# A streaming encoder layer on one core: transposed rows for a triangular solve, 32x32 tiled products, signs on ScalarE, and a head fed by two queues

## The chip, the core and the metric

The kernel runs on one core of one Trainium2 chip. The metric is device time in microseconds (us) of one execution; the time before is the median of three executions. All data are float32. TensorE is called PE below, VectorE DVE, ScalarE ACT, GpSimd POOL and SyncE SP.

## The reference

One layer of a hybrid encoder over 256 time steps of width 2048. Two recurrent mixers (a gated linear recurrence, "LRU", and RWKV-7 with 32 heads of 64) read columns of one input projection; a cross-attention over 256 memory tokens and a SwiGLU follow, each behind a layer norm. Cut to what matters here:

```
h = layer_norm(x, ln_in_g, ln_in_b)
zin = h @ w_in
u, gate_lru, z_rw, g_a, g_b = split(zin)
y_a = gelu(gate_lru) * rg_lru(conv(u))
y_b = rwkv7_time_mix(z_rw)
h = LN1(ALPHA*h + (sig(g_a)*y_a + sig(g_b)*y_b) @ w_out)
h = LN2(ALPHA*h + cross_attention(h, mem))     # k = mem @ wk
h = LN3(ALPHA*h + (silu(h @ wg) * (h @ wu)) @ wd)

# inside rwkv7_time_mix
kf = kf * (1.0 + (a - 1.0) * k_a)
def step(S, inp):
    r_t, w_t, k_t, v_t, kk_t, b_t = inp
    sa = einsum('bhvk,bhk->bhv', S, kk_t)
    S = S * w_t - sa * b_t + v_t * k_t          # outer products per head
    return S, einsum('bhvk,bhk->bhv', S, r_t)
```

The kernel computes the RWKV steps in four chunks of 64 time steps. Within a chunk the steps depend on each other through a unit lower triangular 64x64 matrix per head, and the kernel inverts it.

## The kernel before

**Weights.** Every weight matrix is streamed once, in "halves" of 128x1024 floats (512 KB). `split_half` loads a half on SP's queue (`raw`, L152, four buffers), ACT rounds it to a shorter format (`wh`, L155) and DVE subtracts that from the raw half (`wl`, L157, three buffers for the pair). PE then does eight products of 128x128 with `wh` and 512 columns (L168) and eight with `wl` and 256 columns (L171). Two halves make a 128-wide column block of a projection (`wtile`); ACT copies one part of the sum out of PSUM (`jl`, L183) and DVE adds the other (`js`, `ur`, L186). The output projection, the values, the attention output and the last projection use L202, L203 and L206 with the operands exchanged.

**Stages.** The head loads the memory (`mraw`, L314, four DMAs of 512 KB on SP's queue), splits it in the same manner (ACT L328, DVE L330 into the tiles `m`), computes NB0 = 3 of the 16 key blocks of the cross-attention from it, normalizes x (transposes L256), and computes NB1 = 5 keys in all; these "early keys" are written to DRAM and read back later. Then come four small projections, and four RWKV groups of four 128-wide blocks (eight heads) each, between which the LRU blocks and the gates are placed. After these stand the output projection, the first norm, the cross-attention with the keys that are left, the second norm, the SwiGLU and the last norm.

**The solve of a group.** When the last products of a group (`gt`, L507) are there, `recurrence` writes the 32x32 diagonal blocks of the triangular matrices to DRAM (`scr`, L535) and reads them back as `al`, one system per partition, 32x32 floats each, matrix row index s ahead of column index t (L541). DVE sets the diagonal (L545) and does 31 steps of a triangular inversion: a product `pd` of the part of the inverse that is known with column t of `al` (L552), and a sum over it, `xi` (L555). Element (s, t) of `al` lies 32 floats from (s+1, t), so L552 reads that operand with a stride of 128 bytes. The inverse goes through DRAM once more (`scx`, L558) into `ymat` (L563).

**After the solve.** `chunk_steps` runs when `PACE` (20, 28, 20, 20) more halves have passed. DVE transposes the upper diagonal blocks into `x1z` (L570). PE multiplies them with the off-diagonal blocks (L576), ACT copies the result out (`zz`, L580), PE multiplies with the lower diagonal blocks (L585), and DVE writes the negative of that into `ymat` (L589). `x1z`, `zz` and `ymat` are padded with zeros, so that each 32x32x32 product runs over all 128 rows of the array. Then come four chunks in turn: products L608, ACT copy `rhsz` (L611), products with `ymat` (L615), DVE's negative of that (`sv`, L617), the state (L624 and DVE), products L633 and ACT's copy `ott` (L635). The group norm (L642 is one of its steps) and a gate finish the group.

**Order.** A scheduler sorts each engine's instructions ahead of time by priorities (`tc.cur_priority`, `stream`, `ahead`) and by `defer(n, fn)`, which lets `fn` run after n more halves. On the chip every engine works through its list in that order and waits on semaphores; an instruction that waits holds up all behind it on its engine.

The L552 step reads, with `al` as `[partition, s, t]`:

```
nc.vector.tensor_tensor(pd[:, 0:nj, 0:t + 1], xi[:, 0:nj, 0:t + 1],
                        al[:, 0:t + 1, t].rearrange("p (o s) -> p o s", o=1)
                        .broadcast_to([P, nj, t + 1]), ALU.mult)
nc.vector.tensor_reduce(xi[:, 0:nj, t], pd[:, 0:nj, 0:t + 1], AX.X, ALU.add, negate=True)
```

Of the kernel before, what the change touches and what calls it, by code (L numbers as in the profile page):

```python
# [18 lines left out]
P = 128  # L19
T = 256  # L20
# [11 lines left out]
NB0, NB1 = 3, 5  # L32
XP, CP = 4, 5
# [13 lines left out]
def trunk(ctx, tc, x, memT, vec, rows, consts, lruw, loraw, w_in, w_out, wq, wk, wv, wo, wgu, wd, out,  # L47
# [113 lines left out]

    def wstat(src, xh, xl, acc):
        for hf in range(2):
            h, l = split_half(src, hf)
            for kk in range(8):
                k = hf * 8 + kk
                w = h[:, kk * P:(kk + 1) * P]
                nc.tensor.matmul(acc, w, both[id(xh[k])], start=(k == 0), stop=False)  # L168
            for kk in range(8):
                k = hf * 8 + kk  # L170
                mm = nc.tensor.matmul(acc[:, 0:T], l[:, kk * P:(kk + 1) * P], xh[k], start=False,  # L171
                                      stop=(k == 15))
            passed(mm.ins)
# [4 lines left out]
    def wtile(src, xh, xl, out=None):  # L178
        a = new_acc()
        wstat(src, xh, xl, a)  # L180
        with stream(32):
# [109 lines left out]
    with ExitStack() as mx:  # L291
# [15 lines left out]
        st = wk1.tile([P, 2, 4, 6], F32, name="st")  # L307
        with ahead():
            mraw = []
            for hf in range(2):  # L310
                tc.cur_priority = 65 + hf
                m = boot.tile([P, 8, T], F32, name=f"mraw{hf}")
                for q in range(2):
                    nc.sync.dma_start(m[:, 4 * q:4 * q + 4], memT[:, 8 * hf + 4 * q:8 * hf + 4 * q + 4, :])  # L314
                mraw.append(m)
        tc.cur_priority = 64 * XP + 1
        for tt in range(2):
            for hf in range(2):
                cs = slice(hf * 1024, (hf + 1) * 1024)
                nc.sync.dma_start(xt[:, tt, cs], x[tt * P:(tt + 1) * P, cs])  # L320
        tc.cur_priority = 64 * CP + 2
        nc.sync.dma_start(vt, vec)
        nc.sync.dma_start(ct, consts)
        tc.cur_priority = 1001000
        mTh, mTl = pair_tiles(boot, NK, "m")
        for k in range(NK):
            src = mraw[k // 8][:, k % 8, :]
            nc.scalar.copy(mTh[k], src)  # L328
            eng = nc.gpsimd if k % 4 == 3 else nc.vector
            eng.tensor_tensor(mTl[k], src, mTh[k].bitcast(F32), ALU.subtract)  # L330

# [5 lines left out]
        for k in range(NB0):  # L337
            early_key(k)
# [21 lines left out]
        x1z = grp.tile([P, 2, 16, 32], F32, name="x1z")  # L360
        nc.gpsimd.memset(x1z, 0.0)
        zz = grp.tile([P, 2, 16, 32], F32, name="zz")
        nc.gpsimd.memset(zz, 0.0)
# [78 lines left out]
        def tile_stage(g, j, i, u, fs, av, ev, dt, kr, bkt, sv, yb, gt):  # L442
# [3 lines left out]
            def key_direction():  # L446
# [22 lines left out]
                nc.vector.tensor_scalar(kf, av, col("k_a", i), oka[:, i:i + 1], ALU.mult, ALU.add)  # L469
# [57 lines left out]
        def recurrence(g, kkr, gt, bkt, sv, dm, yb, scr, scx, pace):  # L527
# [17 lines left out]
            nc.vector.memset(al.rearrange("p s t -> p (s t)")[:, 0:1024:33], -1.0)  # L545
# [21 lines left out]
        def chunk_steps(g, kkr, gt, bkt, sv, dm, yb, gi):  # L567
            for pr in range(2):
                q = 64 * (1 - pr)
                nc.vector.transpose(x1z[q:q + 32, pr], ymat[q:q + 32, :, 0:32])  # L570
            psz = rps()
            for pr in range(2):
                q = 64 * (1 - pr)
                for it in range(16):
                    lhsT = gi[:, it // 2, (it % 2) * 2 + pr, q + 32:q + 64]
                    nc.tensor.matmul(psz[q + 32:q + 64, it * 32:(it + 1) * 32], lhsT, x1z[:, pr, it, :],  # L576
                                     start=True, stop=True, skip_group_check=True)
            for pr in range(2):
                q = 64 * (1 - pr)
                nc.scalar.copy(zz[q + 32:q + 64, pr].rearrange("p i t -> p (i t)"), psz[q + 32:q + 64, :])  # L580
            psy = rps()
            for pr in range(2):
                q = 64 * (1 - pr)
                for it in range(16):
                    nc.tensor.matmul(psy[q:q + 32, it * 32:(it + 1) * 32], zz[:, pr, it, :], ymat[:, it, 32:64],  # L585
                                     start=True, stop=True, skip_group_check=True)
            for pr in range(2):
                q = 64 * (1 - pr)
                nc.vector.tensor_scalar(ymat[q:q + 32, :, 32:64],  # L589
                                        psy[q:q + 32, :].rearrange("p (i t) -> p i t", i=16), -1.0, None, ALU.mult)  # L590
# [5 lines left out]
            for c in range(4):  # L596
# [20 lines left out]
                nc.vector.tensor_scalar(sv[q0:q0 + 64, c, :], pss[q0:q0 + 64, :], -1.0, None, ALU.mult)  # L617
# [430 lines left out]
```

## Time and profile before

| what | value |
|---|---|
| time, median of 3 executions | 2145.86 us (2145.09 to 2146.47) |
| the profiled execution's own time | 2147.81 us |
| its span, first to last instruction | 2146.0 us |
| PE busy | 97% of the span |
| DVE busy | 69% |
| ACT busy | 51% |
| POOL busy | 5% |
| mean granted clock of TensorE | 0.991 of full speed |

The span is the time between the first and the last instruction in the profile; the execution's own time is 1.8 us longer. "Busy" is the time in which at least one instruction of an engine was running, and is an average over all stages. A wait is counted for the engine that stood still, and put down to the instruction that released it. In the timeline, a row stands for a run of equal instructions: start, duration from the first start to the last end, engine, line, operation, result and operands, count, and in square brackets the idle time ahead of the row with what ended it. The granted clock of TensorE has two levels, 1.2 and 2.4 GHz; a stretch's PEclk is the mean over it, with 1.00 for 2.4 GHz throughout.

### The profile page before, as it was taken

To read this page: it belongs to the slowest core of one execution; us is meant where nothing else is said; L and a number is where in the kernel's file an instruction comes from. 1 tells how busy PE (TensorE), PEld (TensorE's weight loads), DVE (VectorE), ACT (ScalarE), POOL (GpSimd) and SP (SyncE) were. 2 spreads that over 40 slices of the span, in tenths; PEclk is the share of its full clock that TensorE was granted. 3 is DMA by queue.
4 is the path that set the end of the run, shared out by engine and by line. 5 is a ranking of instruction groups with operands and counts; after the bars stand their busy time and mean duration, and the time that the engine had idled before them with its cause. 6 is when DMAs were issued, how large, how long until landed. Compare 5 with 4: busy or idle time off the path is not lost.

```text
span 2146.0 us, 31754 instructions
## 1 busy us (share of the span) xinstructions
PE 2078.3 (97%) x12176; PEld 1782.4 (83%) x12176; DVE 1472.4 (69%) x2341; ACT 1092.3 (51%) x1658; POOL 117.4 (5%) x162
## 2 busy tenths in 40 slices
PE   7999999999999998999999999999999999999996
PEld 6888788888887887878888888788888888888885
DVE  7888878978795887677864665685555555545545
ACT  6756645565563574564644544454444444443332
POOL 2200010011002000200000000000000000000001
PEclk9999999999999999999999999999999999999998
DMA  8545535544553465386565444565555555555553
GB/s 292 197 157 178 174 111 163 176 145 150 178 175 111 145 189 171 126 280 238 183 210 193 166 142 168 177 217 200 191 187 187 188 190 191 187 190 193 195 192 123
DMA packets 139192, 387.74 MB, mean 181 GB/s; under 512 B 38560, under 2 KB 47648, under 8 KB 138272
## 3 DMA queue, kind: packets, MB, share of 16 engines
q1 hardware_dynamic: 127664, 360.42, 49.4%
q0 software_dynamic: 4384, 14.16, 2.1%
q10 hardware_dynamic: 6992, 11.14, 1.7%
q8 instruction: 95, 1.56, 0.3%
q14 instruction: 57, 0.47, 0.1%
HBM read 375.05 MB, written 10.62 MB: 180 GB/s over the span
## 4 chain that ended last, share of the span: by engine, by line
PE 81%; DVE 10%; DMA 4%; issue 2%; ACT 2%; SPq 0%; POOL 0%; ACTq 0%; DVEq 0%; POOLq 0%
PE acc L168 33%; PE acc L171 17%; PE acc L206 7%; PE acc L202 7%; PE acc L203 7%; DVE wl L157 3%; DVE pd L552 1%; DMA gb<-in_rows_dram 1%; ACT wh L155 1%; DVE xi L555 1%; PE rec L608 1%; PE rec L633 1%; PE rec L615 1%; DMA mraw<-in_memT_dram 1%; PE mix L507 1%
## 5 line engine op out<-in xcount | busy, mean ns | idle before, releaser
L157 DVE TENSOR_TENSOR wl<-raw,wh 128x1024 fp32r<-128x1024 f32 x656 | 801.3, 1223 | 512.8 <-ACT wh L155 485.9
L155 ACT CAST wh<-raw 128x1024 fp32r<-128x1024 f32 x656 | 685.0, 1047 | 651.8 <-PE acc L203 255.7
L168 PE MATMUL acc<-xT,wh 128*128 128x512 f32 x3520 | 914.3, 399 | 10.0 <-DVE js L186 7.7
L168 PEld LDWEIGHTS acc<-xT,wh 128*128 128x128 f32 x3520 | 636.6, 190 | 128.8 <-DVE js L186 9.4
L171 PEld LDWEIGHTS acc<-xT,wl 128*128 128x128 f32 x3520 | 483.0, 191 | 36.4 <-DVE wl L157 0.8
L171 PE MATMUL acc<-xT,wl 128*128 128x256 f32 x3520 | 503.0, 284 | 0.0
L203 PE MATMUL acc<-wh,f 128*128 128x512 f32 x352 | 136.9, 389 | 0.0
L202 PE MATMUL acc<-wh,f 128*128 128x512 f32 x352 | 136.9, 389 | 0.0
L206 PE MATMUL acc<-wl,f 128*128 128x512 f32 x352 | 108.4, 389 | 0.0
L183 ACT COPY jl<-acc 128x256 f32<-128x256 f32 x236 | 86.5, 367 | 24.5 <-PE acc L171 23.8
L186 DVE TENSOR_TENSOR js<-acc,jl 128x256 f32<-128x256 f32 x215 | 89.9, 418 | 5.5 <-ACT jl L183 5.0
L203 PEld LDWEIGHTS acc<-wh,f 128*128 128x128 f32 x352 | 66.1, 188 | 13.8
L206 PEld LDWEIGHTS acc<-wl,f 128*128 128x128 f32 x352 | 66.1, 188 | 13.7
L202 PEld LDWEIGHTS acc<-wh,f 128*128 128x128 f32 x352 | 66.0, 188 | 13.6
L552 DVE TENSOR_TENSOR pd<-xi,al 128x2 f32<-128x2 f32 (+30 forms) x124 | 63.0, 508 | 2.3
L202 PE MATMUL acc<-wh,A 128*128 128x512 f32 x128 | 50.4, 394 | 2.9 <-ACT wh L155 2.9
L203 PE MATMUL acc<-wh,A 128*128 128x512 f32 x128 | 50.3, 393 | 0.0
L202 PE MATMUL acc<-wh,oT 128*128 128x512 f32 x128 | 50.0, 391 | 0.0
L203 PE MATMUL acc<-wh,oT 128*128 128x512 f32 x128 | 49.8, 389 | 0.0
L203 PE MATMUL acc<-wh,B 128*128 128x512 f32 x128 | 49.8, 389 | 0.0
L202 PE MATMUL acc<-wh,B 128*128 128x512 f32 x128 | 49.8, 389 | 0.0
L913 ACT ACTIVATE fsg<-js 128x256 f32<-128x256 f32 x44 | 18.4, 417 | 55.7 <-DVE js L186 55.5
(266 smaller groups left out, 2135.3 us busy)
## 6 DMA issues: line engine op xcount, KB each, us to landing
raw<-in_w_in_dram SPq DMA_DIRECT2D x232, 512.0 KB, 3.5
raw<-in_wgu_dram SPq DMA_DIRECT2D x176, 512.0 KB, 3.5
raw<-in_wd_dram SPq DMA_DIRECT2D x88, 512.0 KB, 3.5
raw<-in_wk_dram SPq DMA_DIRECT2D x32, 512.0 KB, 4.0
raw<-in_w_out_dram SPq DMA_DIRECT2D x32, 512.0 KB, 4.4
raw<-in_wv_dram SPq DMA_DIRECT2D x32, 512.0 KB, 4.0
raw<-in_wq_dram SPq DMA_DIRECT2D x32, 512.0 KB, 3.5
raw<-in_wo_dram SPq DMA_DIRECT2D x32, 512.0 KB, 3.5
```

The source lines that it names most:

```text
L155: nc.scalar.copy(h, raw)
L157: nc.vector.tensor_tensor(l, raw, h.bitcast(F32), ALU.subtract)
L168: nc.tensor.matmul(acc, w, both[id(xh[k])], start=(k == 0), stop=False)
L171: mm = nc.tensor.matmul(acc[:, 0:T], l[:, kk * P:(kk + 1) * P], xh[k], start=False, stop=(k == 15))
L183: nc.scalar.copy(t, a[:, T:2 * T])
L186: nc.vector.tensor_tensor(out, a[:, 0:T], t, ALU.add)
L202: nc.tensor.matmul(pt[tt], xh[k][:, ts], w, start=(first and kk == 0), stop=False)
L203: nc.tensor.matmul(pt[tt], xl[k][:, ts], w, start=False, stop=False)
L206: nc.tensor.matmul(pt[tt], xh[k][:, ts], l[:, kk * 512:(kk + 1) * 512], start=False, stop=(last and kk == 1))
L507: nc.tensor.matmul(pt[hh][:, c * P:(c + 1) * P], q["bk"][rows, c, :], kr[rows, c, :], start=True, stop=True)
L552: nc.vector.tensor_tensor(pd[:, 0:nj, 0:t + 1], xi[:, 0:nj, 0:t + 1], al[:, 0:t + 1, t].rearrange("p (o s) -> p o s", o=1) .broadcast_to([ ...
L555: nc.vector.tensor_reduce(xi[:, 0:nj, t], pd[:, 0:nj, 0:t + 1], AX.X, ALU.add, negate=True)
```

## The change

1. **The solve.** A new tile `at_` holds `al` with s and t exchanged. ACT copies it, all 128x1024 elements, writing with the stride. The diagonal is set in `at_`, and each step reads a row of `at_`, in which neighbours are 4 bytes apart.
2. **The off-diagonal products.** The 32x32 products run in 32x32 tiles of the array (`tile_position`), over 32 rows and without padding. The row pairs alternate product by product, between rows 64 and 0 of the array in the first burst and rows 96 and 32 in the second, and both pairs write one PSUM tile (`psz`, `psy`), as they did before. `x1z` and `zz` give way to one tile `xz`.
3. **Signs and a key step on ScalarE.** The negatives for `ymat` (8 instructions) and `sv` (16), and `kf` = `av` x k_a + oka (16), move from DVE to ACT activations.
4. **The head.** The memory's DMAs are issued on ACT's queue, beside the weights on SP's. Fourteen products of zeros stand at the start of PE's list. Keys 0 and 1 are computed half by half: the first halves of both, which need the first half of the memory alone, and then the second halves. Casts of the memory get priorities between those of the weights, the loads of x are spread between weights, and the small constants change places. NB0 and NB1 become 4 and 7.

```diff
-NB0, NB1 = 3, 5
+NB0, NB1 = 4, 7
...
+        zw = boot.tile([P, P], F32, name="zw")
+        nc.gpsimd.memset(zw, 0.0)
+        zp = rps()
         with ahead():
+            for _ in range(14):
+                nc.tensor.matmul(zp[:, 0:P], zw, zw, start=True, stop=True, skip_group_check=True)
...
-                tc.cur_priority = 65 + hf
+                tc.cur_priority = 65 + 2 * hf
...
-                    nc.sync.dma_start(m[:, 4 * q:4 * q + 4], memT[:, 8 * hf + 4 * q:8 * hf + 4 * q + 4, :])
+                    nc.scalar.dma_start(m[:, 4 * q:4 * q + 4], memT[:, 8 * hf + 4 * q:8 * hf + 4 * q + 4, :])
...
+        krs = [boot.tile([P, T], F32, name="kr", bufs=2) for _ in range(2)]
+        ac = [new_acc() for _ in range(2)]
+        for hf in range(2):
+            for k in range(2):
+                wstat_half(wk[k], mTh, mTl, ac[k], hf)
+        for k in range(2):
+            joined(ac[k], krs[k])
+            nc.sync.dma_start(k_d[k], krs[k])
+        for k in range(2, NB0):
             early_key(k)
...
-                nc.vector.tensor_scalar(kf, av, col("k_a", i), oka[:, i:i + 1], ALU.mult, ALU.add)
+                nc.scalar.activation(kf, av, AF.Identity, scale=col("k_a", i), bias=oka[:, i:i + 1])
...
-            nc.vector.memset(al.rearrange("p s t -> p (s t)")[:, 0:1024:33], -1.0)
+            at_ = grp.tile([P, 32, 32], F32, name="at")
+            nc.scalar.copy(at_.rearrange("p t s -> p s t"), al)
+            nc.vector.memset(at_.rearrange("p t s -> p (t s)")[:, 0:1024:33], -1.0)
...
-                                        al[:, 0:t + 1, t].rearrange("p (o s) -> p o s", o=1)
+                                        at_[:, t, 0:t + 1].rearrange("p (o s) -> p o s", o=1)
...
-                nc.vector.transpose(x1z[q:q + 32, pr], ymat[q:q + 32, :, 0:32])
+                nc.vector.transpose(xz[q:q + 32], ymat[q:q + 32, :, 0:32])
             psz = rps()
+            for it in range(16):
+                for pr in range(2):
+                    q = 64 * (1 - pr)
+                    nc.tensor.matmul(psz[q + 32:q + 64, it * 32:(it + 1) * 32],
+                                     gi[q:q + 32, it // 2, (it % 2) * 2 + pr, q + 32:q + 64], xz[q:q + 32, it, :],
+                                     start=True, stop=True, skip_group_check=True, tile_position=(q, q + 32))
...
-                for it in range(16):
-                    lhsT = gi[:, it // 2, (it % 2) * 2 + pr, q + 32:q + 64]
-                    nc.tensor.matmul(psz[q + 32:q + 64, it * 32:(it + 1) * 32], lhsT, x1z[:, pr, it, :],
-                                     start=True, stop=True, skip_group_check=True)
...
-                nc.vector.tensor_scalar(ymat[q:q + 32, :, 32:64],
-                                        psy[q:q + 32, :].rearrange("p (i t) -> p i t", i=16), -1.0, None, ALU.mult)
+                nc.scalar.activation(ymat[q:q + 32, :, 32:64],
+                                     psy[q:q + 32, :].rearrange("p (i t) -> p i t", i=16), AF.Copy, scale=-1.0)
...
-                nc.vector.tensor_scalar(sv[q0:q0 + 64, c, :], pss[q0:q0 + 64, :], -1.0, None, ALU.mult)
+                nc.scalar.activation(sv[q0:q0 + 64, c, :], pss[q0:q0 + 64, :], AF.Copy, scale=-1.0)
```

The change also moves instructions in the lists. First, SP's queue in the head, where the memory (`mraw`), the weights (`raw`), x (`xt`) and the constants (`ct`, `vt`) are loaded. Before:

```order
L152 DMA raw<-in_wk_dram 128x1024
L314 DMA mraw_150<-in_memT_dram 128x1024
L314 DMA mraw_153<-in_memT_dram 128x1024
L314 DMA mraw_150<-in_memT_dram 128x1024
L314 DMA mraw_153<-in_memT_dram 128x1024
L152 DMA raw<-in_wk_dram 128x1024 x3
L320 DMA xt<-in_x_dram 128x1024 x4
L152 DMA raw<-in_wk_dram 128x1024
```

and with the change, where the four memory loads stand on ACT's queue, ahead of its first cast:

```order
L151 DMA raw<-in_wk_dram 128x1024 x4
L331 DMA xt<-in_x_dram 128x1024 x3
L151 DMA raw<-in_wk_dram 128x1024
L331 DMA xt<-in_x_dram 128x1024
L151 DMA raw<-in_wk_dram 128x1024
L333 DMA ct<-in_consts_dram 128x768
L334 DMA vt<-in_vec_dram 128x356
```

Four weight halves are now issued beside the four memory loads, and not one ahead of them and three behind; a weight half stands ahead of the last load of x.

Second, PE in RWKV group 0, where it comes to the off-diagonal products (`gt` with the transposed blocks `x1z`, later `xz`) between the streamed halves of the blocks behind the group (`xT` with `wh` and `wl`). Before:

```order
L171 MATMUL acc<-xT_95,wl 128x256
L168 MATMUL acc<-xT_80,wh 128x512
L168 MATMUL acc<-xT_81,wh 128x512
L576 MATMUL rec<-x1z,gt 32x32 x16
L168 MATMUL acc<-xT_82,wh 128x512
```

and with the change, later in the list:

```order
L169 MATMUL acc<-xT_86,wl 128x256
L596 MATMUL rec<-xz,gt 32x32
L169 MATMUL acc<-xT_87,wl 128x256
L166 MATMUL acc<-xT_88,wh 128x512
L166 MATMUL acc<-xT_89,wh 128x512
L166 MATMUL acc<-xT_90,wh 128x512
L166 MATMUL acc<-xT_91,wh 128x512
L166 MATMUL acc<-xT_92,wh 128x512
L166 MATMUL acc<-xT_93,wh 128x512
L166 MATMUL acc<-xT_94,wh 128x512
L596 MATMUL rec<-xz,gt 32x32 x31
```

Counted in streamed halves of 16 products, without those of the keys, PE comes to the first of these products after 60.25, 111.0, 163.25 and 214.125 halves in the four groups before, and after 61.0, 111.0, 164.0 and 213.0 with the change.

Third, DVE at the start of group 1's solve, before:

```order
L157 TENSOR_TENSOR wl<-raw,wh 128x1024 x2
L186 TENSOR_TENSOR js<-acc,jl 128x256
L545 MEMSET al 128x32
L552 TENSOR_TENSOR pd<-xi,al 128x2
L555 TENSOR_REDUCE xi<-pd 128x1
```

and with the change:

```order
L156 TENSOR_TENSOR wl<-raw,wh 128x1024 x2
L191 TENSOR_TENSOR js<-acc,jl 128x256
L566 MEMSET at 128x32
L573 TENSOR_TENSOR pd<-xi,at 128x2
L769 TENSOR_TENSOR sb<-sb,yb 128x256
L576 TENSOR_REDUCE xi<-pd 128x1
```

The solve starts behind the same `wl` in group 1; ACT's copy of `al` stands behind the `wh` of the same number in ACT's list. Counted in `wl` without those of the keys, the first `pd` comes after 42, 91, 147 and 194 of them before, and after 43, 91, 147 and 192 with the change; the transposes behind the solve (`x1z`, `xz`) come after 62 to 63, 109, 165 to 166 and 216 to 217, and after 63, 110, 166 and 215.

## Rows read from the trace of the kernel before

**Rows 1.** The page, busy times: engine, us, share of span, instructions; and DVE's largest group.

```profile
PE 2078.3 (97%) x12176; PEld 1782.4 (83%) x12176; DVE 1472.4 (69%) x2341; ACT 1092.3 (51%) x1658; POOL 117.4 (5%) x162
...
L157 DVE TENSOR_TENSOR wl<-raw,wh 128x1024 fp32r<-128x1024 f32 x656 | 801.3, 1223 | 512.8 <-ACT wh L155 485.9
```

**Rows 2.** PE's waits, 170 to 260 us (group 0): total us, times, longest us.

```profile
PE rec L576 <- DVE x1z L570: 2.1, 1, 2.1
PE acc L168 <- DVE js L186: 1.8, 1, 1.8
```

**Rows 3.** The same, 380 to 470 us (group 1).

```profile
PE acc L168 <- DVE js L186: 2.4, 1, 2.4
```

**Rows 4.** The same, 560 to 660 us (group 2).

```profile
PE rec L576 <- DVE x1z L570: 4.0, 1, 4.0
PE acc L168 <- DVE js L186: 1.3, 2, 0.8
```

**Rows 5.** The same, 760 to 900 us (group 3).

```profile
PE rec L576 <- DVE x1z L570: 4.4, 1, 4.4
PE acc L168 <- DVE js L186: 2.2, 2, 1.4
```

**Rows 6.** Busy us by stretch, with PEclk, DMA share and GB/s behind: first and last of four.

```profile
235.00:239.00 4.00, 4.00 (x15) 3.40 (x14) 4.00 (x8) 1.71 (x4) 0.54 (x1) 0.57 0.47 168
...
846.00:854.00 8.00, 5.49 (x44) 4.77 (x44) 4.30 (x8) 2.81 (x7) 0.00 (x0) 0.57 0.68 217
```

**Rows 7.** PE's timeline around the solve of group 0.

```profile
234.69 3.12 PE L168 MATMUL acc<-xT,wh 128*128 128x512 f32 x8 [1.80 <-DVE js L186]
...
239.14 2.02 PE L168 MATMUL acc<-xT,wh 128*128 128x512 f32 x8
...
241.94 2.00 PE L168 MATMUL acc<-xT,wh 128*128 128x512 f32 x8
```

**Rows 8.** Busy time, summed over the four solves (182:240, 374:428, 584:638, 776:839).

```profile
sum 229.00, PE 220.18 PEld 191.24 DVE 220.55 ACT 135.31 POOL 9.16; mean PE 55.04 PEld 47.81 DVE 55.14 ACT 33.83 POOL 2.29
```

**Rows 9.** DVE by line and form: count | busy us, mean ns | idle before, releaser.

```profile
L617 DVE TENSOR_SCALAR sv<-rec 64x512 f32<-64x512 f32 x16 | 11.0, 689 | 26.0 <-PE rec L615 25.7
L469 DVE TENSOR_SCALAR kf<-avg,vt,oka 128x256 f32<-128x256 f32 x16 | 6.5, 406 | 0.0
...
L642 DVE TENSOR_TENSOR ott<-ott,gsm 128x512 f32<-128x512 f32 x8 | 5.5, 691 | 0.1
...
L552 DVE TENSOR_TENSOR pd<-xi,al 128x512 f32<-128x512 f32 x4 | 4.4, 1098 | 0.1
...
L552 DVE TENSOR_TENSOR pd<-xi,al 128x2 f32<-128x2 f32 x4 | 0.6, 161 | 0.1
```

**Rows 10.** ACT by line and form, columns as in 9.

```profile
L611 ACT COPY rhsz<-rec 64x512 f32<-64x512 f32 x16 | 9.3, 582 | 24.5 <-PE rec L608 24.3
...
L409 ACT ACTIVATE evg<-evg 128x1024 f32<-128x1024 f32 x4 | 4.2, 1047 | 0.0
```

**Rows 11.** PE's timeline: an off-diagonal burst, 64-row tiles (L507), full-array products (L624).

```profile
250.29 1.20 PE L576 MATMUL rec<-x1z,gt 128*32 128x32 f32 x32 [2.14 <-DVE x1z L570]
...
165.71 1.16 PE L507 MATMUL mix<-kkr,bk 64*128 64x128 f32 x16
...
263.88 1.05 PE L624 MATMUL rec<-sv,bkt 128*128 128x128 f32 x8
```

**Rows 12.** PE by line and form: the off-diagonal products, all of the first kind.

```profile
L576 PE MATMUL rec<-x1z,gt 128*32 128x32 f32 x256 | 10.5, 206 | 10.5 <-DVE x1z L570 10.5
```

**Rows 13.** PE's timeline in the head.

```profile
6.98 2.08 PE L168 MATMUL acc<-m,wh 128*128 128x512 f32 x4 [6.98 <-DVE m L330]
13.11 2.08 PE L168 MATMUL acc<-m,wh 128*128 128x512 f32 x4 [4.06 <-DVE m L330]
```

**Rows 14.** Busy us by stretch, columns as in 6: the first 20 us.

```profile
0.00:20.00 20.00, 8.96 (x34) 7.14 (x35) 10.51 (x18) 10.75 (x22) 6.62 (x13) 1.00 0.91 331
```

**Rows 15.** SP's timeline: the issue of the memory's loads.

```profile
1.18 1.93 SPq L314 DMA_DIRECT2D mraw<-in_memT_dram  x4
```

More of the change, by code (lines that the diff above doesn't have):

```diff
@@ L31 @@
 PACE = (20, 28, 20, 20)
-NB0, NB1 = 3, 5
-XP, CP = 4, 5
+NB0, NB1 = 4, 7
 ALPHA = float(2.0 ** 0.25)
@@ L160, in trunk, with wstat_half @@
     both, keep = {}, []
+    def wstat_half(src, xh, xl, acc, hf):
+        h, l = split_half(src, hf)
+        for kk in range(8):
+            k = hf * 8 + kk
+            w = h[:, kk * P:(kk + 1) * P]
+            nc.tensor.matmul(acc, w, both[id(xh[k])], start=(k == 0), stop=False)
+        for kk in range(8):
+            k = hf * 8 + kk
+            mm = nc.tensor.matmul(acc[:, 0:T], l[:, kk * P:(kk + 1) * P], xh[k], start=False,
+                                  stop=(k == 15))
+        passed(mm.ins)
     def wstat(src, xh, xl, acc):
         for hf in range(2):
[L164 to L173, printed above, removed]
+            wstat_half(src, xh, xl, acc, hf)
     def new_acc():
@@ L180, in wtile, with joined @@
         wstat(src, xh, xl, a)
+        return joined(a, out)
+    def joined(a, out=None):
         with stream(32):
@@ L327, in trunk @@
             src = mraw[k // 8][:, k % 8, :]
+            tc.cur_priority = 64 * (1 + k // 8) + 17 + k % 8
             nc.scalar.copy(mTh[k], src)
@@ L330, in trunk @@
             eng.tensor_tensor(mTl[k], src, mTh[k].bitcast(F32), ALU.subtract)
+        tc.cur_priority = 1001000
         def early_key(k):
@@ L335, in early_key @@
             nc.sync.dma_start(k_d[k], kr)
-        for k in range(NB0):
+        krs = [boot.tile([P, T], F32, name="kr", bufs=2) for _ in range(2)]
[7 more added lines that the diff above has]
+        for k in range(2, NB0):
             early_key(k)
@@ L359, in trunk @@
             nc.gpsimd.memset(b, 0.0)
[L360 to L363, printed above, removed]
+        xz = grp.tile([P, 16, 32], F32, name="xz")
         ymat = grp.tile([P, 16, 64], F32, name="ymat")
@@ L572, in chunk_steps @@
             for pr in range(2):
                 q = 64 * (1 - pr)
-                for it in range(16):
-                    lhsT = gi[:, it // 2, (it % 2) * 2 + pr, q + 32:q + 64]
-                    nc.tensor.matmul(psz[q + 32:q + 64, it * 32:(it + 1) * 32], lhsT, x1z[:, pr, it, :],
-                                     start=True, stop=True, skip_group_check=True)
+                nc.scalar.copy(xz[q + 32:q + 64].rearrange("p i t -> p (i t)"), psz[q + 32:q + 64, :])
+            psy = rps()
@@ L578, in chunk_steps @@
+            for it in range(16):
+                for pr in range(2):
+                    q = 64 * (1 - pr)
+                    nc.tensor.matmul(psy[q:q + 32, it * 32:(it + 1) * 32], xz[q + 32:q + 64, it, :],
+                                     ymat[q + 32:q + 64, it, 32:64],
+                                     start=True, stop=True, skip_group_check=True, tile_position=(q + 32, q))
             for pr in range(2):
                 q = 64 * (1 - pr)
-                nc.scalar.copy(zz[q + 32:q + 64, pr].rearrange("p i t -> p (i t)"), psz[q + 32:q + 64, :])
@@ L581, in chunk_steps @@
[L581 to L588, printed above, removed]
-                nc.vector.tensor_scalar(ymat[q:q + 32, :, 32:64],
-                                        psy[q:q + 32, :].rearrange("p (i t) -> p i t", i=16), -1.0, None, ALU.mult)
+                nc.scalar.activation(ymat[q:q + 32, :, 32:64],
+                                     psy[q:q + 32, :].rearrange("p (i t) -> p i t", i=16), AF.Copy, scale=-1.0)
```

6 lines of the change are left out of this document (3 added, 3 removed).

## The prediction

> **What bounds the kernel.** I began with the busy times. PE is busy for 97% of the span [rows 1], so a change can gain only what PE stands still, what PE does at less than its full rate, and products that become shorter. DVE's `wl` costs 1,223 ns for each half [rows 1], and a pass of ACT over 128x1024 elements, as a cast is, 1,047 ns [rows 10], both well under the 2.80 us from one half to the next on PE (241.94 - 239.14, [rows 7]). On average, DVE and ACT are therefore no bound.
>
> An average hides the solves. In the four stretches with the triangular loops, DVE is busy for 220.55 of 229.00 us, and ACT for 135.31 [rows 8]. There DVE is late, and PE pays in three ways. It waits for sums `js` that stand behind the loop's steps: 1.8, 2.4, 1.3 and 2.2 us in the groups [rows 2 to 5]. It waits for the transposed blocks `x1z` at the end of the solve: 2.1, 0, 4.0 and 4.4 us [rows 2, 4, 5]. And it loses clock: after the 1.80 us wait of group 0, the next half takes 4.45 us from start to start (239.14 - 234.69) where one takes 2.80 [rows 7], so 1.65 us are lost, and the granted clock of that stretch is 0.57 of full speed, mostly the level of 1.2 GHz; before it fell PE had stood waiting. There are four such stretches, one in each group; the last is of group 3, again at 0.57 [rows 6]. I use 1.65 us for each. At stake are 1.8 + 2.1 + 1.65 = 5.6 us in group 0, 2.4 + 1.65 = 4.1 in group 1, 5.3 + 1.65 = 7.0 in group 2 and 6.6 + 1.65 = 8.3 in group 3: 25.0 us.
>
> The head is the other place: PE starts at 6.98 us, and after four products waits another 4.06 for the second half of the memory [rows 13], while the DMA engines are busy for 0.91 of the first 20 us, at 331 GB/s [rows 14].
>
> **The solve, -18 us.** The largest `pd` has 512 elements per partition and takes 1,098 ns; the product L642, also 512 elements with one operand broadcast, but without a stride, takes 691 [rows 9]. The difference is 0.79 ns per element. The 31 steps have 5,847 elements in all (the sum of (t // 2 + 1)(t + 1)), so reading rows saves 4.65 us per group. The smallest, 2 elements in 161 ns [rows 9], gains nothing, which this sum contains. The key step `kf` takes 0.41 us off DVE for one block that falls beside the loop [rows 9]. Against this stands ACT's copy. No row shows a copy with a strided write: 1.05 us is the price of 128x1024 without a stride [rows 10], and 1.05 x 1098/691 = 1.66 if the stride costs ACT what it costs DVE. I take 1.5, all of it on DVE's path, since the diagonal and the first step wait for it: nearer the upper end, since this copy has a stride. DVE thus gains 4.65 + 0.41 - 1.5 = 3.6 us per group. The order changes what PE allows: in groups 0 and 2 it comes to these products 0.75 half later (61.0 against 60.25, 164.0 against 163.25), 2.1 us at 2.80 per half, while DVE has half a `wl` more to do between the first step and the transposes (0.6 us): 1.5 us net. In group 1 DVE has one `wl` more and PE comes at the same place: -1.2. In group 3 DVE starts two `wl` earlier and PE comes 1.1 halves earlier, so there are 0.9 halves more, 2.5 us, less 0.6. The four gains are 5.1, 2.4, 5.1 and 5.5 of what is at stake, 18.1 us. I take 18. The ends: 9, if only the `x1z` waits shrink by 3.6 (2.1 + 3.6 + 3.6) and the `js` waits and clock losses ahead of them stay, and 25 if all goes.
>
> What is late next in a solve: ACT, which now has the copy in its list of casts, and behind it `wh`. ACT is busy for 59% of these stretches [rows 8], so one copy of up to 1.7 us should be made good.
>
> **The off-diagonal products, -2.4 us.** A burst of 32 records takes 1.20 us [rows 11], the last of it the 0.21 us of one [rows 12], so one starts every 32 ns; 512 of them (256 of each line) are 16.4 us of PE. The columns that stream through do not change, the rows used fall from 128 to 32. Above stands the pitch of 32 ns unchanged, a gain of 0; below, what 64-row tiles show: L507's 16 products in 1.16 us against 8 of L624, on the full array, in 1.05, both with 128 columns [rows 11], 73 ns against 131 if each burst is divided by its count, 0.55, which would save 7.3. I take 2.4, or 15%, nearer the first, since no stream becomes shorter. A loss by the alternation is a rival below.
>
> **The head, -4 us.** While the second half of the memory lands, PE can now do the first halves of two keys and not one. A half is some 2.8 us of PE [rows 7], and the wait it stands in is 4.06 us [rows 13]. With more transfers open at the same time the first half of the memory lands a little later (at 331 GB/s, half a megabyte takes 1.6 us), and PE's very start with it. 2.8 less about 1 of that is some 2. Besides, four products take 2.08 us after each of the two waits [rows 13], as long as eight take later, 2.00 to 2.02 [rows 7], at a granted clock of 1.00 [rows 14]: 1 us is lost at each start. With the products of zeros ahead of the first and a shorter second wait I count both as spared, so 4 in all. The ends are 1 (only what the issue of the loads costs) and 6. The fourteen products of zeros run while PE has nothing else to do, up to the 6.98 us.
>
> Four memory loads take SP 1.93 us to issue [rows 15]; they now leave on ACT's queue beside SP's. The Trainium skill (DMA: Bandwidth & Descriptors, section "Issuing engines are not separate DMA queues") speaks against more than that: transfers share the same 16 engines whoever issues them, and a second issuing engine saves sequencer time only. The share of 0.91 agrees. By the rule alone the head would gain at most 1.9 us, and the sum would be 2 smaller.
>
> **Signs on ACT, +1 us.** The 24 negatives take 689 ns each on DVE [rows 9], and 582 is the nearest ACT row, a copy of the same shape out of PSUM [rows 10]. Each stands between two bursts of products. Where the list of PE has streamed halves between them, this is hidden; where ACT is inside a cast of 1.05 us, the sign starts later. I take +1; the ends are 0 and 8.
>
> **More early keys, +0.5 us.** Two more keys are computed ahead and read back. PE's work is the same; two more small transfers and their places in the lists give 0.5, between -1 and +2. The x loads between weights go together with this.
>
> **Sum.** -18 - 2.4 - 4 + 1 + 0.5 = -22.9 us against the profiled execution's own 2147.81, which is 2124.9. That execution is 1.95 us above the median of the three, 2145.86, so the median of the changed kernel should be **2123**.
>
> **Rivals.** About 0.2% (4.3 us) is what a measurement of this kernel can tell from no change.
>
> *ScalarE becomes the link in the chunks.* Every one of the 24 signs waits in ACT's list for half a cast on average, 0.5 us, and PE's list has no cover: 12 us come back, less the 1 already counted. The result is 2134. For it: ACT already has the copies `rhsz` on the same chain, each of which waits for PE [rows 10]. Against it: DVE was the busier engine, and its `wl` [rows 1] is longer than ACT's pass over as much [rows 10].
>
> *The row read is no faster.* The `pd` of 512 elements stays near 1,098 ns, as it would if the price were the broadcast over an outer index and not the stride. The solve then loses the copy's 1.5 us and gains 0.4 and the places: 0.4, -2.3, 0.4 and 0.8, together about -0.7 (slower), and the sum is -4.2, so about 2141. L642 broadcasts over the inner index, which leaves this open.
>
> *Slower: the alternating tiles take turns.* Two neighbouring products now lie in different rows of the array and write one PSUM bank. If each must end before the other row group starts, one starts every 206 ns [rows 12] and not every 32: 512 x 174 ns = 89 us more, and 2123 + 2.4 + 89 = 2214. It decides the sign from a pitch of about 72 ns, where 512 x 40 ns is the 20.5 us gained elsewhere. For it: the only tiles of part of the rows here, L507, run without such a loss, but with one PSUM tile for each of the two halves of the rows, which `psz` and `psy` don't have. Against it: nothing in the rows shows such a turn. The Trainium skill (TensorEngine Tiling (Array Packing), "Restrictions and Gotchas") says that different row tiles can't access the same PSUM bank at once; no run here shows it, and by that rule this rival is the case.
>
> **The numbers.** The forecast has 0.67, ScalarE 0.16, the row read 0.09, the tiles 0.08. The sum of the lower ends (25 + 7.3 + 6 + 1 for the keys, 0 for ScalarE) is 39 us, 2107. At the upper side the sum of the ends (9, 0, 1, and 8 and 2 given back) comes to no gain, which is too much at once; up to 2140 lie the forecast's bounds and the ScalarE case and part of the row read. The tiles and the rest are left out. Faster by over 0.2%, under 2141.6: 0.83, from the forecast, ScalarE and half of the row read, less a little for bounds that meet. Within it: 0.07. Slower: 0.10.
>
> **What would show it.** The `pd` of 512 elements falls from 1,098 ns to about 690. The `x1z` waits of groups 0, 2 and 3 are under 1 us each, and two or more of the four half-clock stretches are gone. The burst of 32 products takes 1.0 to 1.2 us; over 2.5 us would be the turns. PE's second wait in the head is under 2.5 us and not 4.06. PE waits less than 3 us in all for signs from ACT. The forecast is wrong if the solves' waits stay with a faster loop (then another engine sets when the blocks arrive), or if PE's busy time grows.

## The result and the profile after

The changed kernel takes 2120.36 us (median of 4 executions, 2114.30 to 2121.87) against 2145.48 for the kernel before beside it. The ratio is 0.9875, with a 95% interval from 0.9862 to 0.9889: 1.25% faster. The forecast was 2123. Its profiled execution took 2120.88 us, 26.9 less than the profiled one of before.

The page, busy times and the group that now holds the loop's products:

```profile
PE 2072.1 (98%) x12204; PEld 1779.8 (84%) x12204; DVE 1428.5 (67%) x2301; ACT 1122.0 (53%) x1702; POOL 111.4 (5%) x161
...
L573 DVE TENSOR_TENSOR pd<-xi,at 128x2 f32<-128x2 f32 (+30 forms) x124 | 43.5, 351 | 2.1
```

PE is still the engine that fills the span [rows 1]. It lost 6.2 us of busy time although 5.8 us of products of zeros were added. PE's waits over the whole span: total us, times, longest.

```profile
PE rec L596 <- DVE xz L591: 6.2, 3, 2.6
PE lnt L261 <- DVE hres L255: 5.5, 2, 4.3
PE acc L166 <- DVE m L342: 2.8, 3, 1.7
PE acc L211 <- DVE wl L156: 2.7, 1, 2.7
PE acc L169 <- DVE wl L156: 2.6, 1, 2.6
```

The waits for `js` of the four solves [rows 2 to 5] are gone from the list. The wait for the transposed blocks is 6.2 us, in groups 0, 2 and 3, where it was 10.5. DVE by line and form (count | busy us, mean ns | idle before, releaser), and below it ACT and PE in the same columns:

```profile
L573 DVE TENSOR_TENSOR pd<-xi,at 128x512 f32<-128x512 f32 x4 | 2.7, 685 | 0.0
...
L566 DVE MEMSET at<- 128x32 f32 x4 | 0.3, 85 | 3.7 <-ACT at L565 3.7
```

```profile
L639 ACT ACTIVATE sv<-rec 64x512 f32<-64x512 f32 x16 | 9.5, 591 | 13.6 <-PE rec L637 13.5
...
L565 ACT COPY at<-al 128x1024 f32<-128x1024 f32 x4 | 8.5, 2114 | 0.0
```

```profile
L596 PE MATMUL rec<-xz,gt 32*32 32x32 f32 x256 | 6.3, 203 | 6.2 <-DVE xz L591 6.2
L606 PE MATMUL rec<-ymat,xz 32*32 32x32 f32 x256 | 5.8, 192 | 0.0
```

The largest `pd` takes 685 ns in place of 1,098 [rows 9], and all products of the loop 43.5 us in place of 63.0. ACT's copy takes 2.11 us, and DVE stands 3.7 us in all for it. The off-diagonal products keep PE busy for 12.1 us, where L576 alone took 10.5 [rows 12] and the second burst, L585, 9.3. The two rows of before that this rests on:

```profile
L552 DVE TENSOR_TENSOR pd<-xi,al 128x2 f32<-128x2 f32 (+30 forms) x124 | 63.0, 508 | 2.3
...
L585 PE MATMUL rec<-ymat,zz 128*32 128x32 f32 x256 | 9.3, 197 | 0.0
```

The granted clock by stretch (us, busy us of PE, PEld, DVE, ACT and POOL, PEclk, DMA share, GB/s):

```profile
8.00:16.00 8.00, 6.43 (x18) 4.68 (x19) 2.74 (x7) 3.68 (x10) 1.64 (x3) 0.59 1.03 395
...
20.00:26.00 6.00, 5.63 (x18) 4.86 (x19) 6.00 (x11) 1.47 (x3) 0.00 (x0) 0.50 0.98 368
254.00:262.00 8.00, 6.59 (x97) 5.30 (x96) 7.58 (x15) 5.93 (x10) 0.00 (x0) 1.00 0.73 193
640.00:648.00 8.00, 5.94 (x90) 4.68 (x91) 4.72 (x7) 3.11 (x6) 0.00 (x0) 0.79 0.83 258
826.00:834.00 8.00, 5.40 (x73) 4.32 (x73) 2.96 (x4) 3.09 (x4) 0.00 (x0) 0.67 0.72 211
```

Of the four half-clock stretches in the solves, those of groups 0 and 1 are gone and those of groups 2 and 3 are left in this execution. In a later profile of the same kernel only one is left, in group 0, so which of them stay is not fixed. In the head PEclk, the clock column, is at 0.59 and 0.50, where it reads 1.00 before [rows 14]. That is not a new loss by itself: the four products behind the wait take 2.08 us here (the row at 11.65 below), and they took 2.08 us before as well [rows 13]. PE's timeline there, with the products of zeros first:

```profile
0.99 5.79 PE L319 MATMUL rec<-zw 128*128 128x128 f32 x28 [0.99 <-POOL zw L315]
8.50 0.50 PE L166 MATMUL acc<-m,wh 128*128 128x512 f32 x1 [1.71 <-DVE m L342]
9.37 1.58 PE L166 MATMUL acc<-m,wh 128*128 128x512 f32 x3 [0.37 <-DVE m L342]
11.65 2.08 PE L166 MATMUL acc<-m,wh 128*128 128x512 f32 x4 [0.70 <-DVE m L342]
...
20.37 2.08 PE L169 MATMUL acc<-m,wl 128*128 128x256 f32 x8 [2.62 <-DVE wl L156]
```

The long wait for the memory's second half, 4.06 us [rows 13], is down to 0.70, and 2.62 us of a wait for `wl` have come in its place. DVE's timeline says why:

```profile
18.06 0.69 DVE L232 BATCH_NORM_STATS2 st<-xt 128x6 f32<-128x512 f32 x1 [5.79 <-DMA xt<-in_x_dram]
18.67 1.64 DVE L156 TENSOR_TENSOR wl<-raw,wh 128x1024 fp32r<-128x1024 f32 x1
```

In DVE's list a statistic of x now stands ahead of the second key's `wl`; x lands at 18.06 us, and DVE stands still for 5.79 us with the `wl` behind it.

### The profile page after: what moved, and what is told of

The parts are those of the page before. It is cut to its first block, busy times and chain, and to the rows that moved or that the text cites. A ratio compares the mean times of both kernels' runs of the same rounds, so it can differ in the third digit from the quotient of the medians.

```text
span 2119.0 us, 31844 instructions
## 1 busy us (share of the span) xinstructions
PE 2072.1 (98%) x12204; PEld 1779.8 (84%) x12204; DVE 1428.5 (67%) x2301; ACT 1122.0 (53%) x1702; POOL 111.4 (5%) x161
## 4 chain that ended last, share of the span: by engine, by line
PE 59%; DVE 4%; DMA 3%; issue 2%; ACT 1%; POOL 0%; ACTq 0%; SPq 0%; POOLq 0%; DVEq 0%
PE acc L166 22%; PE acc L169 11%; PE acc L211 7%; PE acc L207 7%; PE acc L208 7%; DVE wl L156 1%; DMA gb<-in_rows_dram 1%; DMA kr<-k_d 1%; ACT wh L154 0%; PE rec L630 0%; PE lnt L261 0%; PE rec L637 0%; PE rec L655 0%; DVE pd L573 0%; DVE xi L576 0%
## 5 line engine op out<-in xcount | busy, mean ns | idle before, releaser
L207 PEld LDWEIGHTS acc<-wh,f 128*128 128x128 f32 x352 | 66.0, 188 | 13.6
L573 DVE TENSOR_TENSOR pd<-xi,at 128x2 f32<-128x2 f32 (+30 forms) x124 | 43.5, 351 | 2.1
```

The costliest lines, as they stand in the source:

```text
L207: nc.tensor.matmul(pt[tt], xh[k][:, ts], w, start=(first and kk == 0), stop=False)
```

## The experiments

**Each part alone.** Four kernels that start from the kernel before. The first has the new products only (part 2 of the diff: `xz` for `x1z` and `zz`, `tile_position`, pairs inside).

> The kernel before with the 32x32 tiles alone (part 2). Theory: shorter bursts are worth what PE's busy time for them falls by, about 4 to 8 us, since PE is the bound in the chunks; the solves' waits stay at about 10 us for the transposed blocks. Expected -3 to -8 us against the kernel before. Rival, the alternating tiles take turns: a burst of 64 records takes over 2.5 us, and the time is not under the kernel before's.

Measured: 2145.34 us, ratio 0.9998 (0.9986 to 1.0009, from 3 us less to 2 us more). No gain that shows. PE's waits of this run, and a stretch of group 1:

```profile
PE rec L572 <- DVE xz L567: 10.3, 3, 4.2
PE acc L168 <- DVE js L186: 8.5, 7, 2.3
...
PE rec L582 <- ACT xz L577: 2.5, 1, 2.5
```

```profile
452.00:460.00 8.00, 7.98 (x97) 6.48 (x98) 2.04 (x3) 2.56 (x4) 0.56 (x2) 0.57 0.16 53
```

The bursts are shorter (12.1 us of PE in place of 19.8), so the rival of turns is out. But in group 1 PE comes to the second burst 2.45 us before ACT's copy of the first is there, a wait that was not in the list before, and the granted clock is 0.57 behind it. PE's busy time falls by 5.8 us in this profile and not by the 7.7 of the bursts, and its span is 3.5 us under that of before; over ten executions nothing is left. That this wait and the clock took the rest is argued from the one profile.

The second has parts 1 and 2 (part 1 alone was not run):

```diff
+            at_ = grp.tile([P, 32, 32], F32, name="at")
+            nc.scalar.copy(at_.rearrange("p t s -> p s t"), al)
...
-                                        al[:, 0:t + 1, t].rearrange("p (o s) -> p o s", o=1)
+                                        at_[:, t, 0:t + 1].rearrange("p (o s) -> p o s", o=1)
```

> Parts 1 and 2 together on the kernel before (part 1 alone has no room in SBUF: its tile takes the place of the padded ones). Theory: the solves gain what the four groups lost, 16 to 20 us, beside the tiles' part: -20 to -26 us against the kernel before, so nearly the whole of the change. Rival, the gain in the solves comes from DVE's other relief (the signs and the key step): not over -10.

Measured: 2124.77 us, ratio 0.9897 (0.9882 to 0.9912), 22 us under the kernel before. This is most of the change. PE's waits for `js` are gone here too, and those for the blocks are

```profile
PE rec L574 <- DVE xz L569: 7.5, 3, 3.2
```

The third has the signs and the key step alone (part 3).

> The kernel before with part 3 alone, the signs and the key step on ScalarE. Theory: DVE's relief beside the solve is one key step of 0.4 us per group, so -3 to +1 us. Rival, DVE's signs held up the chunks: -5 or more. Rival, ScalarE becomes the link: +4 or more.

Measured: 2142.68 us, ratio 0.9977 (0.9966 to 0.9987): 4 us faster (2.8 to 7.3), more than expected, and nothing of a ScalarE that holds the chunks up. The interval reaches into the first rival's range, -5 or more, so that rival is not out. PE's waits:

```profile
PE rec L576 <- DVE x1z L570: 11.7, 3, 4.2
PE acc L168 <- DVE js L186: 5.8, 5, 1.9
```

DVE has 22 us less to do over the span (1450.7 us busy against 1472.4), and the waits for `js` are 1.9 us less; those for the blocks are not. The rest of the 4 us has no single row.

The fourth has the head alone (part 4, with NB0 and NB1).

> The kernel before with part 4 alone, the head. Theory: the head gives 0 to -2 us, because the granted clock is half the full speed from 12 to 26 us, where it stayed full in the head before, and that takes back what the shorter waits give; the clock falls here too. Rival: the head gives its 4 us and the rest of the changed kernel lost them: -3 to -6.

Measured: 2144.76 us, ratio 0.9988 (0.9977 to 0.9999), some 2 us (0.2 to 4.9). The clock column falls here too, 0.60 against 1.00 before:

```profile
8.00:16.00 8.00, 6.58 (x19) 4.70 (x20) 2.79 (x7) 3.71 (x10) 1.82 (x3) 0.60 1.02 393
```

That it takes gain back, as the theory had it, is not shown; the products' durations, below, speak against it.

The four medians stand beside one median of the kernel before, 2146.95: -22.2 for the solves with the products, -4.3 for the signs, -2.2 for the head, 28.7 in all. The whole change gave 25.1 in its first runs, and 29.1 in a later pair (2117.46 against 2146.60).

**Does the row read do it, or the place in PE's list?** The changed kernel came to the products 0.75 half later in two groups, so the gain of the solves could be the scheduler's. This kernel keeps PE's list as it is in the changed kernel (on DVE one `js` stands one place earlier, in group 0) and takes away only the exchange:

```diff
-            nc.scalar.copy(at_.rearrange("p t s -> p s t"), al)
+            nc.scalar.copy(at_, al)
...
-                                        at_[:, t, 0:t + 1].rearrange("p (o s) -> p o s", o=1)
+                                        at_[:, 0:t + 1, t].rearrange("p (o s) -> p o s", o=1)
```

> The changed kernel with its copy made without the exchange: ACT copies the tile as it is, and the loop reads columns of the copy, at a stride of 128 bytes. The list of every engine is the same as in the changed kernel. Theory: reading rows makes the loop faster, so the largest product is near 1,098 ns again, DVE loses 4.65 us per group less about 1 that the plain copy saves, and 4 x 3.6 = 14 us come back: about 2134. Rival, the place in PE's list makes the gain: at most 4 us come back, up to 2124.

Measured: 2133.71 us, ratio 0.9943 (0.9921 to 0.9964). 13 us come back against the first time of the changed kernel, 2120.36. On this run's own chip stood the changed kernel without the products of zeros, 2115.31 (below), and against it 18 us. The theory said 14, and the rival's 2124 lies below all executions. DVE and ACT by form, and PE's waits, from this run's slowest execution (2140.78):

```profile
L573 DVE TENSOR_TENSOR pd<-xi,at 128x512 f32<-128x512 f32 x4 | 4.5, 1136 | 0.0
```

```profile
L565 ACT COPY at<-al 128x1024 f32<-128x1024 f32 x4 | 4.2, 1044 | 0.0
```

```profile
PE rec L596 <- DVE xz L591: 9.6, 3, 3.5
...
PE acc L166 <- DVE js L191: 4.9, 6, 1.7
```

The `js` waits are back with the slow loop. The copy without the exchange takes 1.04 us, so the strided write costs ACT 1.07 us per group.

**What shortens the bursts?** The same tiles, with one row pair after the other:

```diff
-            for it in range(16):
-                for pr in range(2):
-                    q = 64 * (1 - pr)
+            for pr in range(2):
+                q = 64 * (1 - pr)
+                for it in range(16):
```

> The changed kernel with the 32x32 products of one row pair first and then those of the other, so that neighbours lie in the same rows of the array. Theory: what shortens a burst is the smaller tile, not the alternation, and no turns were taken: a burst of 64 records takes 1.2 us as with the alternation, and the time is within 3 us of the changed kernel's. Rival, neighbours in different rows overlap: the burst takes 2.0 us (32 ns from start to start) as before, and 4 us come back.

Measured: 2133.06 us, ratio 0.9928 (0.9912 to 0.9945): 13 us slower than the first time of the changed kernel and 18 slower than the 2115.31 on the same chip. The theory fell, and the rival was right in kind and too small. The scheduler also puts a few streamed products elsewhere between the bursts, which this run does not part from the order of the pairs. In its slowest execution (2138.88), the one that was profiled, PE by form, the burst of group 1 in the timeline, and group 0's chunk by stretch:

```profile
L606 PE MATMUL rec<-ymat,xz 32*32 32x32 f32 x256 | 13.1, 220 | 0.0
L596 PE MATMUL rec<-xz,gt 32*32 32x32 f32 x256 | 11.4, 208 | 4.8 <-DVE xz L591 4.8
```

```profile
451.91 2.11 PE L596 MATMUL rec<-xz,gt 32*32 32x32 f32 x64
```

```profile
258.00:268.00 10.00, 10.00 (x99) 8.36 (x96) 4.14 (x8) 2.26 (x4) 0.00 (x0) 0.54 0.33 111
```

A burst of 64 records takes 2.11 us, where the alternating one takes 1.20:

```profile
446.12 1.20 PE L596 MATMUL rec<-xz,gt 32*32 32x32 f32 x64
```

The smaller tile alone gains nothing: with neighbours in the same rows, a record starts every (2.11 - 0.21) / 63 = 30 ns, as with the padded products [rows 11]. With neighbours in other rows, two share that time. Over the kernel the bursts cost 24.5 us in place of 12.1. At 30 ns and full speed they would cost about 17 (512 x 0.030 and 0.21 for each of eight ends); the rest is clock, which is at half for longer in the chunks of groups 0, 2 and 3 here (0.54, above). The changed kernel's same stretch of group 0 is at full speed in its first profile:

```profile
258.00:268.00 10.00, 10.00 (x185) 8.32 (x184) 6.43 (x12) 6.45 (x11) 0.00 (x0) 1.00 0.55 172
```

and at 0.66 in the later one:

```profile
258.00:268.00 10.00, 10.00 (x161) 8.13 (x161) 5.41 (x10) 3.67 (x6) 0.00 (x0) 0.66 0.32 107
```

**One PSUM tile or two?** The changed kernel with `psz = [rps(), mps()]` and the same for `psy`, indexed by the pair.

> The changed kernel with the two row pairs in two PSUM tiles. In group 1's first burst the products still alternate between rows 64 and 0; in the others the scheduler puts one pair ahead of the other. Theory: alternating row groups overlap whether they write one bank or two, so group 1's first burst takes 1.2 us as with one bank, and the bursts that don't alternate start a record every 32 ns. Rival, one bank costs turns: with two banks the burst takes clearly less, 0.8 us or under.

Measured in one execution: 2126.72 us. The scheduler parted the pairs in all bursts but one. In group 1's first burst they alternate, and its 64 records run from 450.11 to 451.31, 1.20 us as with one tile (first and last row):

```profile
450.11 0.21 PE L596 MATMUL rec<-xz,gt 32*32 32x32 f32 x1
...
451.12 0.19 PE L596 MATMUL mix<-xz,gt 32*32 32x32 f32 x1
```

A burst with the pairs parted takes as long for half the records:

```profile
260.69 1.19 PE L596 MATMUL mix<-xz,gt 32*32 32x32 f32 x32
```

So the alternation is what shortens a burst, and one PSUM bank for both pairs costs nothing that shows, by this one burst with two banks.

**The products of zeros.** First put into the kernel before:

```diff
+        zw = boot.tile([P, P], F32, name="zw")
+        nc.gpsimd.memset(zw, 0.0)
+        zp = rps()
...
+            for _ in range(14):
+                nc.tensor.matmul(zp[:, 0:P], zw, zw, start=True, stop=True, skip_group_check=True)
```

> The kernel before with the fourteen products of zeros at the start of PE's list, and nothing else. Theory: the granted clock, full in the whole head before, falls to half in the first 30 us, and the first halves take about twice their time. Rival: the clock stays full, and the other parts of the new head make it fall.

Measured in one execution: 2152.79 us, against a median of 2146.02 for the kernel before beside it, whose own executions reach 2150.45. The clock column falls twice in the head, where it reads 1.00 before:

```profile
12.00:16.00 4.00, 2.83 (x9) 2.32 (x10) 3.14 (x6) 3.60 (x9) 2.35 (x3) 0.50 1.03 410
...
28.00:36.00 8.00, 7.12 (x25) 6.07 (x26) 5.05 (x18) 3.52 (x6) 0.00 (x0) 0.57 0.29 88
```

But the first halves do not take twice their time, as the theory had it. The four products at 13.17 us take 2.07 us, and took 2.08 before [rows 13]. The second fall does slow PE, and it follows a wait of 3.01 us for ACT's `wh`, where the kernel before waits 1.41 us. In this run's list on ACT a copy `jl`, which waits for PE, stands ahead of a table load and the first `rs`, and that `wh` starts at 27.79 us in place of 25.68. So the second fall can't be put down to the zeros.

Then taken out of the changed kernel, first by itself, and then with the changed kernel beside it on the same chip.

> The changed kernel without the fourteen products of zeros. Theory: they put PE to work ahead of the waits of the head, and the granted clock falls to half from 12 to 26 us; without them it stays at full speed there, as in the head before, and the time is 2 to 5 us less than the changed kernel's. Rival: the clock falls anyway, because the waits of the head do it: 0 to +2 us.

Measured: 2115.31 us, ratio 0.9851 (0.9836 to 0.9867), 5 us less than the first time of the changed kernel, which was not measured beside it.

> The changed kernel as it is, beside the next run on the same chip. Expected 2117 to 2122 us, as before.

> The changed kernel without the fourteen products of zeros, beside the run above. Theory: the 5 us that the first pair of runs showed hold, 2113 to 2117. Rival: the first profile puts only 0.7 us of them into the head, where the loads set the time, so they were another chip's or other executions': within 2 us of the run above.

Measured side by side: 2117.46 us with the products (0.9870, 0.9854 to 0.9887) and 2117.29 without (0.9863, 0.9848 to 0.9878). The 5 us did not hold. Without them the clock column reads 1.00 up to 20 us, and 0.72 in the 6 us behind:

```profile
8.00:16.00 8.00, 6.98 (x23) 4.94 (x24) 2.85 (x7) 3.79 (x10) 1.83 (x3) 1.00 1.03 396
...
20.00:26.00 6.00, 5.83 (x26) 5.14 (x27) 6.00 (x11) 2.33 (x4) 0.00 (x0) 0.72 1.03 372
```

PE's timeline of the same run does not bear the 1.00 out:

```profile
11.46 2.08 PE L166 MATMUL acc<-m,wh 128*128 128x512 f32 x4 [0.34 <-DVE m L336]
...
14.53 2.00 PE L166 MATMUL acc<-m,wh 128*128 128x512 f32 x8
```

Four products take 2.08 us and, 3 us later, eight of the same shape take 2.00, all under a column of 1.00. The four take just as long with the zeros, at 0.59. So in the first products of the head PE runs at half its later rate with the zeros and without, and the column there is no measure of it.

The small projections behind the head begin at 83.02 us with the zeros and 82.95 without in this pair of profiles, and at 83.82 and 83.14 in the first two. PE's wait for that `wl` is 2.62 and 2.79 us with them, and 2.36 and 3.64 without. The zeros gain and cost nothing that shows.

**A version that goes on.** Without the products of zeros, with the copy in two pieces and the off-diagonal products later:

```diff
-PACE = (20, 28, 20, 20)
+PACE = (28, 28, 28, 28)
...
-            nc.scalar.copy(at_.rearrange("p t s -> p s t"), al)
+            for lo, hi in ((0, 8), (8, 32)):
+                nc.scalar.copy(at_[:, lo:hi, 0:hi].rearrange("p t s -> p s t"), al[:, 0:hi, lo:hi])
```

(The diagonal is set in two pieces as well.)

> Without the products of zeros; ACT's copy in two pieces (8 rows that the first steps need, then 24), and PACE (28, 28, 28, 28), which puts the off-diagonal products of groups 0 and 2 two and three halves later in PE's list. Theory: what is left of the solves' cost is DVE's wait for the copy (0.9 us of each group) and PE's waits of 1.4, 2.2 and 2.6 us with half-clock stretches behind the last two; DVE starts a good 1 us earlier, and the waits of groups 0 and 2 go: 4 to 8 us less than the run above. Rival: later products push the chunks behind them into the next stage, which waits for them instead: no gain.

Measured: 2113.68 us, ratio 0.9853 (0.9838 to 0.9868), the lowest median of all kernels here and 3.8 us under the changed kernel beside it; the intervals overlap, so that it beats the changed kernel is likely and not settled. Against the same kernel without zeros beside it, 2117.29, it gives 3.6, a little under the 4 to 8 of the theory. DVE's waits for the copy are gone, and PE's for the blocks are left in group 3 alone; two others are larger than in the changed kernel beside it:

```profile
L570 DVE MEMSET at<- 128x24 f32 x4 | 0.3, 78 | 0.0
L562 DVE MEMSET at<- 128x8 f32 x4 | 0.3, 65 | 0.0
```

```profile
PE rec L687 <- DMA lwg<-in_loraw_dram: 4.3, 4, 2.5
...
PE mix L465 <- ACT sq L463: 2.2, 2, 1.8
PE rec L594 <- DVE xz L589: 1.3, 1, 1.3
```

Both theory and rival hold in part: the waits that were aimed at went, and PE now waits for ACT's square in a key step (1.8 us, in group 2) and a little longer for the gate's small load (4.3 against 3.7 us).

## Why the prediction came out right, point by point

**The bound.** Right: PE's waits in the solves were DVE's, and a faster loop took them away. Taking the stretch by itself, and not DVE's 69% of the span, found the place.

**The solve, -18.** By the same count as in the prediction, 25.0 us were at stake; 6.2 us of waits and two half-clock stretches, 3.3 us, are left, so 15.5 were gained. The loop's products fell by 63.0 - 43.5 = 19.5 us, 4.9 per group where the prediction had 4.65, so the price per element (0.79 ns, from L642) was right; the row-read rival is out. The single step of reading columns again, with PE's list unchanged, gives 13 to 18 us back where the prediction's own numbers said 14. The bound on the copy failed. It was put between 1.05 and 1.66 us and is 2.11: a strided write slows ACT by a factor of 2.0 (2.11 against 1.04 us), a strided read slows DVE by 1.6 (1,098 against 685 ns). DVE's waits are 3.7 us in four groups all the same, and not 8.5, since DVE has other work while ACT copies; the 1.5 us per group on DVE's path were too many. Of what would show it, the waits of the blocks are 1.4, 2.2 and 2.6 us and not under 1.

**The products, -2.4.** The step that failed is the choice of a value near "no gain". The other end, from L507, gave 7.3, and 7.7 us is what PE's busy time for the bursts fell by (19.8 - 12.1); as a gain in time this was not measured, since the tiles alone gave none. L507 was the nearest row after all, since it alternates between two row groups as the new code does. The argument that no stream becomes shorter was true, and missed that two streams run side by side. The prediction's "burst of 32 products" is a burst of 32 records, two to a product; 64 records now take the 1.20 us, so the 1.0 to 1.2 us that it expected to see for 32 was off by the same step.

**The turns (the slower rival).** Out, at 1.20 us for a burst where it needed some 13 for 64 records. The rule of the Trainium skill (TensorEngine Tiling (Array Packing), "Restrictions and Gotchas"), that different row tiles can't access one PSUM bank at once, doesn't show here: row tiles that alternate on one bank, 64 records in 1.20 us, run as fast as on two, and nearly twice as fast as without alternation (2.11). Where page and measurement differ, the measurement decides.

**The head, -4.** Measured in the first profile, it is about -0.4: the first product of the small projections behind the head starts at 83.82 us in place of 73.04, 10.8 later, with four more halves of keys ahead of it, 4 x 2.80 = 11.2. In the later profile it starts at 83.02, which makes -1.2. The memory's wait went as foreseen. Two steps failed. The first is that the list of DVE was not followed: the statistic of x stands ahead of the second key's `wl`, x lands at 18.06, and PE waits 2.62 us. The second is the 2 us counted as spared at the two starts: behind the zeros the first four products still take 0.50 and 1.58 us, and the next four 2.08, as before [rows 13]. PE's start on the memory also came 1.5 us later (8.50 against 6.98), where the prediction allowed about 1. Alone, the head gave 2.2 us, between 0.2 and 4.9 by its interval. By the rule of the Trainium skill (DMA: Bandwidth & Descriptors, "Issuing engines are not separate DMA queues") the gain would be at most the 1.9 us of issue; the runs don't contradict that. A kernel with the statistics behind that `wl` was not tried.

**Signs, +1.** The sign of the term was wrong: alone they gave -4.3. The 13.6 us for which ACT stands ahead of `sv` are idle time of ACT, not of PE. PE's list does have streamed halves between the chunk's products, and no wait for a sign stands among its larger ones. ScalarE as the link in the chunks is out. Where their 4.3 us come from stays open; a row shows only 1.9 us of `js` waits.

**The sum.** -15.5 for the solves, -7.7 for the bursts and -0.4 for the head are 23.6 of the 26.9 us; the remaining 3.3 are nearly what the signs gave alone. A sum of 22.9 was close because the bursts, too small by 5, and the signs, off by 5, made good for the head and the solve, too large by 3.6 and 2.5. That these errors cancelled is luck; that the solves make up most of the change is not. The split is a count in one profile of each kernel.

## What to carry to other kernels

An engine with a share of 69% can be the bound for 50 us at a time; look at the stretches in which PE waits, and there at operands with a stride: a copy by an engine with time to spare, 2.1 us for each of four groups, is worth 13 to 18 us of the kernel. Small products gain from tiling the array only if neighbours in the list lie in different row groups; check that the scheduler keeps them so. Shorter products alone gave no time here. When transfers are brought forward, read each consumer's list for an instruction that waits for the later of them.

## What was not expected of the hardware

For the first products of the head the clock column is no measure of PE's rate. It reads 1.00 in the kernel before and in the changed one without the products of zeros, and 0.59 with them, and in all three the four products behind the memory's second wait take 2.08 us, where eight of them later take 2.00. Products of zeros at the start of PE's list left these durations as they were, and the time too (2117.46 us with, 2117.29 without).

With one row pair after the other, the granted clock was at half for longer in the chunks (0.54 over 10 us in group 0, 0.52 over 16 in group 3), behind waits of 1.7 and 1.0 us. The alternating kernel showed 1.00 and 0.66 in that stretch of group 0 in two executions, so that the order of the products was the cause is not shown. ACT pays more for a stride of 128 bytes on its output (2.11 against 1.04 us) than DVE for one on its input (1,136 against 685 ns).
